# One tile for each PSUM bank, low parts one step later, weight sums one step earlier and a copy moved ahead, in the second feed-forward layer of an encoder step

## The chip, the cores and the metric

The kernel runs on one core of a Trainium2 chip. The metric is the device time of one execution in microseconds (us); smaller is better. Five engines work side by side and wait for each other by semaphores: PE (TensorE, matmuls, with its weight loads shown as PEld), DVE (VectorE), ACT (ScalarE), POOL (GpSimd) and SP (SyncE, which issues the DMA transfers). Matmul results land in PSUM, eight banks of 512 f32 in each of 128 partitions.

## The reference

One layer of a streaming encoder: a SwiGLU feed-forward layer, two attention mixers side by side and a second SwiGLU layer, for 1024 prompt frames and 32 sample frames with 1024 features. The change concerns the second feed-forward layer, on 1056 columns in all:

```
def swiglu(h, w_gate, w_up, w_down):
    return (jax.nn.silu(h @ w_gate) * (h @ w_up)) @ w_down

    h = adaln_in(x, gains[4], sh3, sc3)
    x = x + FFN_RES * g3[:, None] * rmsnorm(swiglu(h, w2_gate, w2_up, w2_down), gains[5])
```

The hidden width is 2816, all data is f32.

## The kernel before

Every matrix product is made of three matmuls of a faster f32 form: each operand is split into a high part (ACT, a copy that rounds) and a low part (DVE, operand minus high part), and the product is high x high + high x low + low x high. A split of 128x512 weights is lines 535 (ACT) and 536 (DVE), in `pair_of`.

The columns are cut into three blocks of 384, 384 and 288. The hidden width is cut into 11 groups of 256. A round takes one group through a gate stage (`g`), an up stage (`u`) and a down stage (`d`); the order of the stages is interleaved, so that round r's down stage follows the gate stage of round r + 1: g(r+1), d(r), u(r+1), g(r+2) and so on. The first two groups are done block by block (six rounds, function `plain`), the other nine for all blocks at once (function `strassen`).

In `strassen` the weights of the group are a 2 x 2 matrix of blocks A11, A12, A21, A22 (128 hidden by 512 input features each), and the first two column blocks with the two halves of the input features form a 2 x 2 matrix too. Seven products in place of eight give the result, with weight sums S1 = A21 + A22, S2 = S1 - A11, S3 = A11 - A21, S4 = A12 - S2 (`Mat.of`, line 559, on DVE) and sums of the input T1 to T4 that are made once. The products run in the order A11, A12, S2, S1, S3, A22, A21, S4. A11, A12, A22 and A21 also make an ordinary product with the third column block (tile `g`, 288 columns); A21 has only that one. The banks are: `a` for A11 and then A12 on top of it, `b` for S2 and then S3, `d` for S1 and then S4, `e` for A22, `0` and `1` for the third block. After A11 the bank `a` is copied out (line 756, ACT), and A12 is added to it. DVE reads `b` after S2, `b` and `d` after S3, `e` after A22 and `d` after S4 (line 741), and `made` turns each finished block into silu (gate, line 688) or into the product with the gate and its split (up: lines 692 on DVE, 693 on ACT, 694 on DVE, tile `gg`).

PSUM is handed out by three pools: `ps2` (two buffers of two banks; before: `b` and `d` together as tile `gu`, the third block's `g`, and the down stage's `dn`), `ps1` (three buffers of one bank; before: `a` and `e`, both named `ge`) and `psc` (one bank). Waits are kept per tile. In SBUF, raw weights have four buffers (tag `r`), split weights four (tag `w`).

The order of the instructions on PE, ACT and DVE is the order of the program from the gate stage of the eighth round (round 7, counted from 0) to the last gate stage (`manual_schedule`); elsewhere a scheduler orders them. In the program, step n of `strassen` splits the weights of products n + 1 and n + 2 before it issues product n; `nexts` loads the next stage's weights after the first product and splits its first ones after the sixth. Low parts are issued right behind their high parts.

Of the kernel before, what the change touches and what calls it, by code (L numbers as in the profile page):

```python
# [10 lines left out]
AF = mybir.ActivationFunctionType  # L11
OP = mybir.AluOpType
# [66 lines left out]
def encoder_step(ctx: ExitStack, tc, x_prompt, x_sample, cache_a_k, cache_a_v, cache_b_k, cache_b_v,  # L79
# [41 lines left out]
    def p2(name, shape=(128, 2, 512)):  # L121
        return ps2.tile(list(shape), F32, name=name, tag="p2")
# [4 lines left out]
    def p1(name, shape=(128, 512)):  # L127
        return ps1.tile(list(shape), F32, name=name, tag="p1")
# [400 lines left out]
        yield from norm_h(f, tb, j + 1, H)  # L529


    def pair_of(src):

        w = t_tile("w", [128, 2, 4, 128], "w", F32R)
        ae.activation(w[:, 0], src, AF.Copy)  # L535
        ve.tensor_tensor(w[:, 1], src, w[:, 0], op=OP.subtract)  # L536
        return w[:, 0], w[:, 1]

    class Mat:
# [19 lines left out]
                ve.tensor_tensor(a[name], x, y, op=op)  # L559
            return a[name]  # L560

        def split(self, name):
            if name not in self.done:
                self.done[name] = pair_of(self.of(name))
            return self.done[name]

    class Rows:
# [9 lines left out]
        def split(self, q, hf):  # L577
            if (q, hf) not in self.w:
                self.w[q, hf] = pair_of(self.raw[q][:, 4 * hf:4 * hf + 4])

    def product(ps, w, x, first, last):
        n = len(x[0])
        for k in range(n):
            for q, (a, b) in enumerate(((0, 0), (0, 1), (1, 0))):
                te.matmul(ps, w[a][:, k, :], x[b][k], start=first and k == 0 and q == 0,  # L585
                          stop=last and k == n - 1 and q == 2, skip_group_check=True)
# [58 lines left out]
    def ffn(key, H, tags, F, facc, wg, wu, wd, key_out, after, beside):  # L645
# [18 lines left out]
            else:  # L664
                loaded[r, what] = Mat((wg, wu)[what == "u"], gi)

        def ready(i):

            if i >= len(stages):
                return  # L670
            load(i)
            r, what = stages[i]
            m = loaded[r, what]
            if what == "d":
                m.split(0, 0)
                m.split(1, 0)
            else:
                m.split("A11")
                if r not in fast or what == "u":
                    m.split("A12")  # L680

        def made(r, what, f, tb, src):

            w = TB[tb][1]
            if what == "g":
                if (r, f, tb) not in sl:
                    sl[r, f, tb] = s_tile([128, 384], "sl")[:, :w]
                ae.activation(sl[r, f, tb], src, AF.Silu)  # L688
# [3 lines left out]
            ve.tensor_tensor(v, v, src, op=OP.mult)  # L692
            ae.activation(g[:, 0, :w], v, AF.Copy)
            ve.tensor_tensor(g[:, 1, :w], v, g[:, 0, :w], op=OP.subtract)  # L694

        def half(tb, d):
            return [e[4 * d:4 * d + 4] for e in H[tb][:2]]

        def plain(r, what, m, tbs, beside, early=None):
            n = 0  # L700
            for f in range(2):
                w_ = [m.split(f"A{f + 1}{d + 1}") for d in range(2)]
                if f and early:
                    early()
                for tb in tbs:
                    w = TB[tb][1]
                    ps = p1("gate" if what == "g" else "up")
                    for d in range(2):
                        product(ps[:, :w], w_[d], half(tb, d), d == 0, d == 1)
                        if f == 0:  # L710
                            m.split(f"A2{d + 1}")
                    made(r, what, f, tb, ps[:, :w])
                    beside(n)
                    n += 1
                    step(STEPS)

        def strassen(r, what, m, two, beside):
            w, w2 = 384, TB[2][1]
            B = {"B11": half(0, 0), "B21": half(0, 1), "B22": half(1, 1), **T}
            banks, v = {}, {}  # L720

            def bank(name):
                if name not in banks:
                    if name in "bd":
                        t = p2("gu")
                        banks["b"], banks["d"] = t[:, 0, :w], t[:, 1, :w]
                    elif name in "01":
                        t = p2("g2")
                        banks["0"], banks["1"] = t[:, 0, :w2], t[:, 1, :w2]
                    else:  # L730
                        banks[name] = p1("ge")[:, :w]
                return banks[name]

            def temp(name, f, tb):
                v[name] = s_tile([128, 384], "sl" if what == "g" else "ut")
                if what == "g":
                    sl[r, f, tb] = v[name]
                return v[name]

            def plus(out, b, x):  # L740
                ve.tensor_tensor(out, banks[b], v[x], op=OP.add)

            seq = [x for x in STRASSEN if two or x[1]]
            for n, (name, x, at, blk2) in enumerate(seq):
                w_ = m.split(name)
                for nx in seq[n + 1:n + 3]:
                    m.split(nx[0])
                if name == "S3":
                    m.of("S4")
                if x:  # L750
                    product(bank(at), w_, B[x], name in ("A11", "S2", "S1", "A22"), True)
                if two and blk2:
                    f, d = int(name[1]) - 1, int(name[2]) - 1
                    product(bank(str(f)), w_, half(2, d), name in ("A11", "A22"), True)
                if name == "A11":
                    ae.activation(temp("s", 1, 0), banks["a"], AF.Copy)
                elif name == "A12":
                    made(r, what, 0, 0, banks["a"])
                elif name == "S2":
                    plus(temp("u", 0, 1), "b", "s")  # L760
                elif name == "S3":
                    plus(v["s"], "b", "s")
                    plus(temp("c", 1, 1), "d", "s")
                    made(r, what, 1, 1, v["c"])
                elif name == "A22":
                    plus(v["s"], "e", "s")
                    made(r, what, 1, 0, v["s"])
                elif name == "S4":
                    plus(v["u"], "d", "u")
                    made(r, what, 0, 1, v["u"])  # L770
                elif name == "A21":
                    made(r, what, 0, 2, banks["0"])
                    made(r, what, 1, 2, banks["1"])
                beside(n)
                step(pace)

        owns = {}

# [36 lines left out]
        steady = ExitStack()  # L815
        for i, (r, what) in enumerate(stages):
            gi, blocks = plan[r]
            if (r, what) == (min(fast) + 1, "g"):
                steady.enter_context(tc.manual_schedule(engines=INLINE))
            if (r, what) == (len(plan) - 1, "u"):  # L820
                steady.close()
            load(i)
            m = loaded[r, what]

            def nexts(n, last, i=i):
                if n == 0:
                    load(i + 1)
                elif n == last:
                    ready(i + 1)

            if what == "d":
                for q in range(2):
                    m.split(q, 0)
                order = list(blocks)
                ending = any(r == final[tb] for tb in order)
                todo = [(tb, mp) for tb in order for mp in range(4)] if ending else \
                    [(tb, mp) for h in range(2) for tb in order for mp in (2 * h, 2 * h + 1)]
                for n, (tb, mp) in enumerate(todo):
                    if n == 1:
                        for q in range(2):  # L840
                            m.split(q, 1)
                    nexts(n, len(todo) - 3)
                    down(r, tb, m, mp)
            elif r in fast:
                need((key, "T"))
                strassen(r, what, m, 2 in blocks, lambda n: nexts(n, 5))
            else:
                for tb in blocks:
# [3 lines left out]
                load(i + 1)  # L852
                plain(r, what, m, blocks, lambda n: None, lambda: ready(i + 1))
            if what == "u" and gi == NF // 2 - 1:
                beside()


    GROUPS = [list(range(g, min(g + 2, NF))) for g in range(0, NF, 2)]

# [807 lines left out]
    def beside():  # L1667
        for t in (1, 0, 2):
            begin(("xp", t), tokens_first(t))
# [36 lines left out]
```

## Time and profile before

| | us |
|---|---|
| median of 3 runs (lowest, highest) | 2240.74 (2239.55, 2245.29) |
| the profiled execution | 2239.8 |
| its span, first to last instruction | 2238.0 |
| block products (first to last matmul of `ge` and `gu`) | 1559.0 to 2182.9 |

The granted TensorE clock over the span is 0.98 of full speed. How to read the rows below: a group has its line, engine, operation, out<-in and count. A row of waits has who waited, for whom, the total, the number of times and the longest. A row in order of time has its start, its length, engine, line and operation, and in brackets how long the engine had stood idle and what released it. The chain of work that ended last has the start, the length and the work on it.

### The profile page before, as it was taken

The page shows a single profiled execution, that of the slowest core. Times are in us where ns is not written, and L with a number is a line of the kernel's source. Part 1 is how long each engine was busy: PE and PEld are TensorE (multiplying, and loading weights), DVE is VectorE, ACT ScalarE, POOL GpSimd, SP SyncE. Part 2 cuts the span into 40 slices and gives each one's busy share as a digit, 9 for nine tenths or more (in the row PEclk, how much of TensorE's full clock was granted, in tenths as well). Part 3 has the DMA queues.
Part 4 walks back from the last instruction along what each step waited for, and adds up shares of the span by engine and source line. Part 5 has one row for each costly group of instructions (what it writes and reads, how often), then busy time and mean ns, then how long its engine had stood idle before and what let it go on. Part 6 is the DMA issues. An engine that isn't in the chain of part 4 may idle for free.

```text
span 2238.0 us, 34284 instructions
## 1 busy us (share of the span) xinstructions
PE 2141.4 (96%) x13796; PEld 2041.0 (91%) x13796; DVE 1406.3 (63%) x2783; ACT 783.3 (35%) x1654; POOL 173.4 (8%) x273
## 2 busy tenths in 40 slices
PE   6999999999999999999999999999999999999997
PEld 4999999999999998898787589999999889998897
DVE  5778667774333596677445866787555555555558
ACT  4412111111111344567445663555322222222224
POOL 1100000000000122001112323210000000000001
PEclk9999999999999999899999999999999999999999
DMA  9244334443121352111103032444211111111114
GB/s 316 99 148 134 102 86 134 129 124 103 40 75 57 118 179 77 37 39 30 54 25 103 5 95 76 144 127 131 62 52 38 57 38 39 55 40 38 38 57 137
DMA packets 178804, 192.35 MB, mean 86 GB/s; under 512 B 7789, under 2 KB 147477, under 8 KB 177493
## 3 DMA queue, kind: packets, MB, share of 16 engines
q1 hardware_dynamic: 178644, 190.16, 27.4%
q8 instruction: 108, 1.77, 0.3%
q14 instruction: 52, 0.42, 0.1%
HBM read 170.42 MB, written 22.86 MB: 86 GB/s over the span
## 4 chain that ended last, share of the span: by engine, by line
PE 83%; DVE 9%; DMA 3%; ACT 3%; issue 1%; POOL 0%; SPq 0%; DVEq 0%; ACTq 0%; POOLq 0%
PE gu L585 6%; PE ge L585 4%; PE g L585 4%; PE up L341 4%; PE gate L341 4%; PE up L340 4%; PE up L339 4%; PE gate L340 4%; PE dn L339 4%; PE dn L340 3%; PE dn L341 3%; PE gate L339 3%; PE dn L795 3%; PE dn L797 3%; PE dn L796 3%; PE po L1060 3%
## 5 line engine op out<-in xcount | busy, mean ns | idle before, releaser
L318 DVE TENSOR_TENSOR w<-raw,w 128x1024 fp32r<-128x1024 f32 x109 | 135.1, 1244 | 81.0 <-ACT w L317 80.1
L795 PE MATMUL dn<-gg,w 128*128 128x384 f32 (+1 forms) x528 | 170.4, 324 | 2.9 <-ACT sl L688 1.4
L382 POOL TENSOR_TENSOR sq<-sq 128x384 f32<-128x384 f32 (+1 forms) x48 | 53.0, 1114 | 1548.0 <-ACT sq L378 1518.3
L339 PE MATMUL dn<-gg,w 128*128 128x384 f32 (+1 forms) x528 | 169.8, 323 | 1.2 <-DVE facc L928 1.1
L796 PE MATMUL dn<-gg,w 128*128 128x384 f32 (+1 forms) x528 | 169.3, 321 | 1.8 <-DVE gg L694 1.8
L340 PE MATMUL dn<-gg,w 128*128 128x384 f32 (+1 forms) x528 | 169.6, 321 | 0.6 <-DVE gg L901 0.6
L341 PE MATMUL dn<-gg,w 128*128 128x384 f32 (+1 forms) x528 | 169.4, 321 | 0.0
L797 PE MATMUL dn<-gg,w 128*128 128x384 f32 (+1 forms) x528 | 168.9, 322 | 0.4 <-DVE w L536 0.4
L317 ACT ACTIVATE w<-raw 128x1024 fp32r<-128x1024 f32 x109 | 114.5, 1056 | 146.0 <-PE up L341 48.8
L535 ACT ACTIVATE w<-raw 128x512 fp32r<-128x512 f32 x180 | 109.0, 624 | 153.7 <-issue 76.0
L802 DVE TENSOR_TENSOR facc<-dn,facc 128x768 f32<-128x768 f32 (+1 forms) x120 | 106.6, 890 | 87.8 <-PE dn L797 87.8
L928 DVE TENSOR_TENSOR facc<-dn,facc 128x768 f32<-128x768 f32 (+1 forms) x120 | 106.1, 887 | 81.3 <-PE dn L341 81.3
L243 DVE SCALAR_TENSOR_TENSOR macc<-raw,csil,macc 128x512 f32<-128x512 f32 x196 | 137.6, 746 | 14.7 <-DMA raw<-in_w_mod_dram 14.4
L536 DVE TENSOR_TENSOR w<-raw,w 128x512 fp32r<-128x512 f32 x180 | 122.8, 706 | 25.1 <-ACT w L535 24.8
L585 PE MATMUL gu<-t,w 128*128 128x384 f32 x648 | 119.7, 336 | 11.2 <-ACT w L535 11.2
L897 ACT ACTIVATE sl<-gate 128x384 f32<-128x384 f32 (+1 forms) x66 | 30.5, 463 | 281.7 <-PE gate L341 278.9
L585 PE MATMUL g<-h_hi,w 128*128 128x288 f32 x576 | 125.8, 298 | 0.0
L585 PEld LDWEIGHTS gu<-t,w 128*128 128x128 f32 x648 | 111.3, 188 | 15.6 <-issue 8.3
L340 PE MATMUL gate<-h,w 128*128 128x384 f32 x352 | 118.0, 335 | 1.9 <-DVE h L467 1.9
L339 PE MATMUL gate<-h,w 128*128 128x384 f32 x352 | 118.3, 336 | 0.0
L341 PE MATMUL gate<-h,w 128*128 128x384 f32 x352 | 117.9, 335 | 0.0
L341 PE MATMUL up<-h,w 128*128 128x384 f32 x352 | 117.9, 335 | 0.0
(314 smaller groups left out, 5820.7 us busy)
## 6 DMA issues: line engine op xcount, KB each, us to landing
raw<-in_w_gate_dram SPq DMA_DIRECT2D x58, 512.0 KB, 4.0
raw<-in_w_up_dram SPq DMA_DIRECT2D x58, 512.0 KB, 4.0
raw<-in_w_down_dram SPq DMA_DIRECT2D x58, 512.0 KB, 3.6
raw<-in_w_mod_dram SPq DMA_DIRECT2D x56, 512.0 KB, 3.9
raw<-in_w_in_dram SPq DMA_DIRECT2D x18, 512.0 KB, 4.2
wm<-in_w_mod_dram SPq DMA_DIRECT2D x8, 1024.0 KB, 7.1
raw<-in_w_out_dram SPq DMA_DIRECT2D x13, 512.0 KB, 4.5
xr<-xs SPq DMA_DIRECT2D x16, 384.0 KB, 3.6
```

Of the source, the lines that this page charges most:

```text
L243: ve.scalar_tensor_tensor(acc[j], r[:, kk], c, acc[j], op0=OP.mult, op1=OP.add)
L317: ae.activation(w[:, 0], r, AF.Copy)
L318: ve.tensor_sub(w[:, 1], r, w[:, 0])
L339: te.matmul(ps, w[:, 0, k], hi, start=start, stop=False)
L340: te.matmul(ps, w[:, 0, k], lo, start=False, stop=False)
L341: te.matmul(ps, w[:, 1, k], hi, start=False, stop=stop)
L535: ae.activation(w[:, 0], src, AF.Copy)
L536: ve.tensor_tensor(w[:, 1], src, w[:, 0], op=OP.subtract)
L585: te.matmul(ps, w[a][:, k, :], x[b][k], start=first and k == 0 and q == 0, stop=last and k == n - 1 and q == 2, skip_group_check=True)
L795: te.matmul(ps[:, s, :w], h[:, k % 4, :], g[:, 0, :w], start=q == 0, stop=False)
L796: te.matmul(ps[:, s, :w], h[:, k % 4, :], g[:, 1, :w], start=False, stop=False)
L797: te.matmul(ps[:, s, :w], l[:, k % 4, :], g[:, 0, :w], start=False, stop=q == 1)
```

## The change

`pair_of` and `made` no longer issue the low part on DVE at once but put it into a list, which `flush` issues at the end of the step. In `strassen`, banks `a`, `b` and `d` are tiles of `ps1` of their own (`ga`, `gb`, `gd`) and `e` is the tile of `psc`. Each step issues its product first; after A11 the copy of bank `a` comes next (new line 774), then the high part of the weights two products on, then the reading of the product before (`after_product`), then the low parts, then the weight sum for the product three on. The next stage's first two weights are split in the last two steps, one each. Down stages take the same form. Loads are issued at the start of a stage. The part in program order begins one round earlier, at the first gate stage in block products.

```diff
+    deferred = []
+
+    def flush():
+        while deferred:
+            deferred.pop(0)()
+
     def pair_of(src):
         w = t_tile("w", [128, 2, 4, 128], "w", F32R)
         ae.activation(w[:, 0], src, AF.Copy)
-        ve.tensor_tensor(w[:, 1], src, w[:, 0], op=OP.subtract)
+        deferred.append(lambda: ve.tensor_tensor(w[:, 1], src, w[:, 0], op=OP.subtract))
         return w[:, 0], w[:, 1]
...
             ae.activation(g[:, 0, :w], v, AF.Copy)
-            ve.tensor_tensor(g[:, 1, :w], v, g[:, 0, :w], op=OP.subtract)
+            deferred.append(lambda: ve.tensor_tensor(g[:, 1, :w], v, g[:, 0, :w], op=OP.subtract))
...
-                    if name in "bd":
-                        t = p2("gu")
-                        banks["b"], banks["d"] = t[:, 0, :w], t[:, 1, :w]
-                    elif name in "01":
+                    if name in "01":
                         t = p2("g2")
                         banks["0"], banks["1"] = t[:, 0, :w2], t[:, 1, :w2]
                     else:
-                        banks[name] = p1("ge")[:, :w]
+                        banks[name] = (pc if name == "e" else p1)("g" + name)[:, :w]
...
-            seq = [x for x in STRASSEN if two or x[1]]
-            for n, (name, x, at, blk2) in enumerate(seq):
-                w_ = m.split(name)
-                for nx in seq[n + 1:n + 3]:
-                    m.split(nx[0])
-                if name == "S3":
-                    m.of("S4")
+            names = [x[0] for x in STRASSEN]
+            for n, (name, x, at, blk2) in enumerate(STRASSEN):
+                w_ = m.done[name]
                 if x:
                     product(bank(at), w_, B[x], name in ("A11", "S2", "S1", "A22"), True)
...
-                if name == "A11":
-                    ae.activation(temp("s", 1, 0), banks["a"], AF.Copy)
-                elif name == "A12":
...
-                beside(n)
+                if n == 0:
+                    ae.activation(temp("s", 1, 0), banks["a"], AF.Copy)
+                if n < 6:
+                    m.begin(names[n + 2])
+                else:
+                    early(n - 6)
+                if n:
+                    after_product(names[n - 1])
+                flush()
+                if n < 5:
+                    m.of(names[n + 3])
                 step(pace)
+            after_product(names[-1])
...
-            if (r, what) == (min(fast) + 1, "g"):
+            if (r, what) == (min(fast), "g"):
+                need((key, "T"))
                 steady.enter_context(tc.manual_schedule(engines=INLINE))
...
             load(i)
             m = loaded[r, what]
+            load(i + 1)
```

Here is ACT where the up stage of round 13 ends and the last gate stage begins, before. `w<-raw` and `w<-ws` are high parts of weights (`ws` is a weight sum), `gg<-sl` high parts of the hidden activations, `sl<-ge` at L756 is the copy of bank `a`; the names after "waits" are the engines waited for.

```order
L693 ACTIVATE gg<-sl 128x288 [waits DVE_49] x2
L693 ACTIVATE gg<-sl 128x384 [waits DVE_49]
L535 ACTIVATE w<-raw 128x512 [waits DMAHW3_49,PE_49,Activation_49]
L535 ACTIVATE w<-ws 128x512 [waits DVE_49,PE_49,Activation_49]
L756 ACTIVATE sl<-ge 128x384 [waits PE_49]
L535 ACTIVATE w<-ws 128x512 [waits Activation_49]
```

And ACT at the same place now; the copy is `sl<-ga` at L774.

```order
L541 ACTIVATE w<-raw 128x512 [waits DMAHW1_49,PE_49,Activation_49]
L699 ACTIVATE gg<-sl 128x288 [waits DVE_49] x2
L699 ACTIVATE gg<-sl 128x384 [waits DVE_49]
L774 ACTIVATE sl<-ga 128x384 [waits PE_49]
L541 ACTIVATE w<-ws 128x512 [waits DVE_49,Activation_49]
L541 ACTIVATE w<-ws 128x512 [waits Activation_49]
```

The copy has moved ahead of the split of S2 (the first `w<-ws`), and the split of A12 (`w<-raw`) ahead of the up stage's last high parts.

DVE at the same boundary, before, from the third block's products with the gate to the low part of S2.

```order
L692 TENSOR_TENSOR sl<-sl,g_19778 128x288 [waits PE_49]
L694 TENSOR_TENSOR gg<-sl,gg 128x288 [waits Activation_49]
L692 TENSOR_TENSOR sl<-sl,g_19778 128x288
L694 TENSOR_TENSOR gg<-sl,gg 128x288 [waits Activation_49]
L741 TENSOR_TENSOR ut<-gu,ut 128x384 [waits PE_49]
L692 TENSOR_TENSOR sl<-sl,ut 128x384 [waits DVE_49]
L694 TENSOR_TENSOR gg<-sl,gg 128x384 [waits Activation_49]
L536 TENSOR_TENSOR w<-raw,w 128x512 [waits DMAHW1_49,Activation_49]
L559 TENSOR_TENSOR ws<-raw 128x512
L559 TENSOR_TENSOR ws<-ws,raw 128x512 [waits DVE_49]
L536 TENSOR_TENSOR w<-ws,w 128x512 [waits Activation_49] x2
```

And DVE there now.

```order
L698 TENSOR_TENSOR sl<-sl,g_19789 128x288 [waits PE_49]
L698 TENSOR_TENSOR sl<-sl,g_19789 128x288
L542 TENSOR_TENSOR w<-raw,w 128x512 [waits DMAHW1_49,Activation_49]
L700 TENSOR_TENSOR gg<-sl,gg 128x288 [waits Activation_49] x2
L744 TENSOR_TENSOR ut<-gd,ut 128x384 [waits PE_49]
L698 TENSOR_TENSOR sl<-sl,ut 128x384 [waits DVE_49]
L565 TENSOR_TENSOR ws<-raw 128x512
L565 TENSOR_TENSOR ws<-ws,raw 128x512 [waits DVE_49]
L700 TENSOR_TENSOR gg<-sl,gg 128x384 [waits Activation_49]
L542 TENSOR_TENSOR w<-ws,w 128x512 [waits Activation_49] x2
```

The low parts (L536, L694; now L542, L700) stand later, with a product or a weight sum between them and the high part that they wait for.

PE in a gate stage before, from A12's product with the third block to S3: `gu<-t_14999` is S2 into bank `b`, `gu<-t_14998` is S1 into bank `d`, `gu<-t_14997` is S3 into bank `b`.

```order
L585 MATMUL gu<-t_14999,w 128x384 [waits DVE_49]
L585 MATMUL gu<-t_14999,w 128x384
L585 MATMUL gu<-t_14999,w 128x384 [waits DVE_49]
L585 MATMUL gu<-t_14999,w 128x384 x9
L585 MATMUL gu<-t_14998,w 128x384 [waits DVE_49,Activation_49]
L585 MATMUL gu<-t_14998,w 128x384 x11
L585 MATMUL gu<-t_14997,w 128x384 [waits Activation_49]
L585 MATMUL gu<-t_14997,w 128x384 x11
```

And PE at the same place now, in tiles `gb` and `gd`.

```order
L595 MATMUL gb<-t_14999,w 128x384 [waits Activation_49]
L595 MATMUL gb<-t_14999,w 128x384
L595 MATMUL gb<-t_14999,w 128x384 [waits DVE_49]
L595 MATMUL gb<-t_14999,w 128x384 x9
L595 MATMUL gd<-t_14998,w 128x384 [waits Activation_49]
L595 MATMUL gd<-t_14998,w 128x384
L595 MATMUL gd<-t_14998,w 128x384 [waits DVE_49]
L595 MATMUL gd<-t_14998,w 128x384 x9
L595 MATMUL gb<-t_14997,w 128x384 [waits DVE_49,Activation_49]
L595 MATMUL gb<-t_14997,w 128x384 x11
```

The first matmul of S1 waited for DVE and now waits for ACT alone (S1's high part); DVE's low part is waited for by the third matmul, which is the first to use it. The wait for DVE's reading of bank `b` stands at S3, which writes that bank.

More of the change, by code (lines that the diff above doesn't have):

```diff
@@ L560, in of, with begin, split @@
             return a[name]
-        def split(self, name):
+        def begin(self, name):
             if name not in self.done:
                 self.done[name] = pair_of(self.of(name))
+        def split(self, name):
+            self.begin(name)
+            flush()
             return self.done[name]
@@ L575, in __init__, with begin @@
                 self.raw.append(r)
-        def split(self, q, hf):
+        def begin(self, q, hf):
             if (q, hf) not in self.w:
@@ L671, in ready @@
             load(i)
[L672 to L676, printed above, removed]
-            else:
-                m.split("A11")
-                if r not in fast or what == "u":
-                    m.split("A12")
+            m = loaded[stages[i]]
+            if stages[i][1] == "d":
+                m.begin(piece, 0)
+            else:
+                m.begin(("A11", "A12")[piece])
         def made(r, what, f, tb, src):
@@ L693, in made, with plain @@
             ae.activation(g[:, 0, :w], v, AF.Copy)
-            ve.tensor_tensor(g[:, 1, :w], v, g[:, 0, :w], op=OP.subtract)
+            deferred.append(lambda: ve.tensor_tensor(g[:, 1, :w], v, g[:, 0, :w], op=OP.subtract))
         def half(tb, d):
             return [e[4 * d:4 * d + 4] for e in H[tb][:2]]
-        def plain(r, what, m, tbs, beside, early=None):
-            n = 0
+        def plain(r, what, m, tbs, early):
             for f in range(2):
                 w_ = [m.split(f"A{f + 1}{d + 1}") for d in range(2)]
-                if f and early:
-                    early()
+                if f:
+                    early(0)
+                    early(1)
+                    flush()
                 for tb in tbs:
@@ L712, in plain, with strassen @@
                     made(r, what, f, tb, ps[:, :w])
-                    beside(n)
-                    n += 1
+                    flush()
                     step(STEPS)
-        def strassen(r, what, m, two, beside):
+        def strassen(r, what, m, early):
             w, w2 = 384, TB[2][1]
@@ L741, in plus, with after_product @@
                 ve.tensor_tensor(out, banks[b], v[x], op=OP.add)
-            seq = [x for x in STRASSEN if two or x[1]]
-            for n, (name, x, at, blk2) in enumerate(seq):
-                w_ = m.split(name)
-                for nx in seq[n + 1:n + 3]:
-                    m.split(nx[0])
-                if name == "S3":
-                    m.of("S4")
[L750 to L754, printed above, removed]
-                if name == "A11":
-                    ae.activation(temp("s", 1, 0), banks["a"], AF.Copy)
-                elif name == "A12":
+            def after_product(name):
+                if name == "A12":
                     made(r, what, 0, 0, banks["a"])
@@ L767, in strassen @@
                     made(r, what, 1, 0, v["s"])
+                elif name == "A21":
+                    made(r, what, 0, 2, banks["0"])
+                    made(r, what, 1, 2, banks["1"])
                 elif name == "S4":
@@ L770, in strassen @@
                     made(r, what, 0, 1, v["u"])
[L771 to L774, printed above, removed]
+            names = [x[0] for x in STRASSEN]
+            for n, (name, x, at, blk2) in enumerate(STRASSEN):
+                w_ = m.done[name]
+                if x:
+                    product(bank(at), w_, B[x], name in ("A11", "S2", "S1", "A22"), True)
+                if blk2:
+                    f, d = int(name[1]) - 1, int(name[2]) - 1
+                    product(bank(str(f)), w_, half(2, d), name in ("A11", "A22"), True)
+                if n == 0:
[6 more added lines that the diff above has]
+                    after_product(names[n - 1])
+                flush()
+                if n < 5:
+                    m.of(names[n + 3])
                 step(pace)
+            after_product(names[-1])
         owns = {}
@@ L823, in ffn @@
             m = loaded[r, what]
[L825 to L829, printed above, removed]
+            load(i + 1)
             if what == "d":
+                ending = any(r == final[tb] for tb in blocks)
+                todo = [(tb, mp) for tb in blocks for mp in range(4)] if ending else \
+                    [(tb, mp) for h in range(2) for tb in blocks for mp in (2 * h, 2 * h + 1)]
                 for q in range(2):
[L833 to L837, printed above, removed]
-                for n, (tb, mp) in enumerate(todo):
[L839 to L842, printed above, removed]
+                    m.begin(q, 0)
+                for n, (tb, mp) in enumerate(todo):
+                    flush()
+                    if n < 2:
+                        m.begin(n, 1)
+                    if n >= len(todo) - 2 and r in fast or r not in fast and n >= 2:
+                        ready(i + 1, n % 2)
                     down(r, tb, m, mp)
             elif r in fast:
-                need((key, "T"))
-                strassen(r, what, m, 2 in blocks, lambda n: nexts(n, 5))
+                for name in ("A11", "A12"):
+                    m.begin(name)
+                strassen(r, what, m, lambda k: ready(i + 1, k))
             else:
+                flush()
                 for tb in blocks:
@@ L851, in ffn @@
                     begin((key, "T"), combos(H, T, tags))
-                load(i + 1)
-                plain(r, what, m, blocks, lambda n: None, lambda: ready(i + 1))
+                plain(r, what, m, blocks, lambda k: ready(i + 1, k))
             if what == "u" and gi == NF // 2 - 1:
                 beside()
+        flush()
     GROUPS = [list(range(g, min(g + 2, NF))) for g in range(0, NF, 2)]
```

2 lines of the change are left out of this document (1 added, 1 removed).

## The prediction

> **What bounds the kernel now.** I read the busy shares of the page first, then who TensorE (PE) waited for in the second feed-forward layer, then one round of that layer on each engine, and last the granted clock around its longest wait.
>
> ```profile
> PE 2141.4 (96%) x13796; PEld 2041.0 (91%) x13796; DVE 1406.3 (63%) x2783; ACT 783.3 (35%) x1654; POOL 173.4 (8%) x273
> 460.00:660.00 200.00, 200.00 (x1254) 199.83 (x1253) 97.28 (x167) 34.56 (x53) 0.00 (x0) 1.00 0.30 90
> 1844.00:1916.00 72.00, 67.03 (x409) 66.21 (x409) 39.73 (x63) 17.71 (x34) 0.00 (x0) 0.98 0.14 45
> PE ge L585 <- ACT sl L756: 24.3, 7, 3.5
> PE gu L585 <- ACT w L535: 11.2, 15, 0.8
> PE dn L795 <- ACT sl L688: 1.4, 2, 0.8
> ```
>
> The first row is the page's busy list: TensorE is the bound, and DVE (VectorE) and ACT (ScalarE) have room. The next two are the table of stretches (length, busy time of PE, PEld, DVE, ACT and POOL, granted clock, DMA share, GB/s). The first feed-forward layer runs TensorE without a gap at clock 1.00; a 72 us stretch of the second, which is about one round, leaves 5 us idle at clock 0.98. The last three are all that TensorE waited for between 1559 and 2183 us, the part in block products: 7 waits of the second product (A12, tile `ge`) for the copy of line 756, and 15 waits on `gu`. Only what shortens these moves the end.
>
> One round, followed back along the chain of work that ended last (start, length, what):
>
> ```profile
> 1900.12 3.83 PE ge L585 x12
> 1903.94 1.59 PE g L585 x12
> 1905.53 2.10 PE gu L585 x12
> 1908.36 4.40 PE gu L585 x24
> 1920.11 0.17 PE dn L795
> 1943.08 2.08 PE ge L585 x12
> 1945.15 1.59 PE g L585 x12
> 1972.15 3.67 PE L585 MATMUL ge<-h,w 128*128 128x384 f32 x12 [3.47 <-ACT sl L756]
> ```
>
> (The last row is from the order of time.) An undisturbed product of 12 matmuls takes 2.08 us at 384 columns and 1.59 us at 288. A gate or up stage has seven of the first and four of the second, 20.92 us; the down stage lasts from 1920.11 to 1943.08, 22.97 us. A round of gate, down and up is then 2 x 20.92 + 22.97 = 64.81 us of work. It took 1972.15 - 1900.12 = 72.03 us. The missing 7.2 us are what the change is aimed at, and they split as follows.
>
> **Part 1, the copy at the head of ACT's order.** Around the same boundary from up to gate:
>
> ```profile
> 1966.69 0.55 DVE L741 TENSOR_TENSOR ut<-gu,ut 128x384 f32<-128x384 f32 x1
> 1967.28 0.56 DVE L692 TENSOR_TENSOR sl<-sl,ut 128x384 f32<-128x384 f32 x1
> 1967.87 0.52 ACT L693 ACTIVATE gg<-sl 128x384 fp32r<-128x384 f32 x1 [1.59 <-DVE sl L692]
> 1968.30 0.61 ACT L535 ACTIVATE w<-raw 128x512 fp32r<-128x512 f32 x1
> 1968.95 0.69 DVE L536 TENSOR_TENSOR w<-raw,w 128x512 fp32r<-128x512 f32 x1
> 1970.28 0.69 DVE L559 TENSOR_TENSOR ws<-ws,raw 128x512 f32<-128x512 f32 x1
> 1971.09 0.63 ACT L535 ACTIVATE w<-ws 128x512 fp32r<-128x512 f32 x1 [2.17 <-DVE ws L559]
> 1971.62 0.47 ACT L756 ACTIVATE sl<-ge 128x384 f32<-128x384 f32 x1
> ```
>
> TensorE had finished A11 and its second-block product at 1972.15 - 3.47 = 1968.68. A12 adds into the same bank and must wait until line 756 has copied it out. The copy itself is 0.47 us, but it stands behind the split of S2, which waited 2.17 us for DVE, which was still working off the up stage. With the copy ahead of that split the 3.47 us go, 24.3 us in seven boundaries. What follows the wait is slow too:
>
> ```profile
> 1900.00:1902.00 2.00, 1.89 (x6) 1.89 (x7) 1.70 (x3) 0.58 (x2) 0.00 (x0) 0.50 0.00 0
> 1902.00:1904.00 2.00, 2.00 (x10) 2.00 (x9) 0.00 (x0) 0.02 (x1) 0.00 (x0) 0.66 0.00 0
> 1682.72 4.21 PE ge L585 x12
> 1686.92 2.27 PE g L585 x12
> 2117.38 3.40 PE ge L585 x12
> 2120.78 2.12 PE g L585 x12
> ```
>
> The granted clock is 0.50 in the two microseconds after the wait. The pairs shown are the first and last of seven; over all seven A12 and the product after it took 40.4 us against 7 x 3.67 = 25.7, so 14.7 us more go with the wait. [...]
>
> Is the copy early enough in the new order? Count from the end of S3's product, with the durations above and DVE's pitch of 0.6 us: two sums out of PSUM, a product with the gate, S4's low part, a low part of `gg`, the sum on `e` with its product, A11's low part, `gg`, make 5.2 us; A21's product ends at 2.08 + 1.59 + 1.59 = 5.26. Then two products at 0.4, A12's low part, two low parts at 0.4: 7.5, after S4's end at 7.34. Sum and product for block 0,1: 8.7; ACT's high copy 0.53: 9.2. A11 ends at 7.34 + 2.08 = 9.42, the copy at 9.9, and A12 can start at 11.0. **1.1 us to spare.** S2's weights come from the two sums (10.0), the split on ACT (10.6) and its low part (11.3), and are wanted at 14.7. So the cover is there; if DVE were later than this by x us, each of the seven boundaries would lose x - 1.1.
>
> **Part 2, a tile for each bank.**
>
> ```profile
> 1907.66 0.56 DVE L741 TENSOR_TENSOR sl<-gu,sl 128x384 f32<-128x384 f32 x1 [1.94 <-PE gu L585]
> 1907.71 0.63 ACT L535 ACTIVATE w<-raw 128x512 fp32r<-128x512 f32 x1 [1.46 <-PE gu L585]
> 1908.36 4.40 PE L585 MATMUL gu<-t,w 128*128 128x384 f32 x24 [0.74 <-ACT w L535]
> 1959.47 0.52 ACT L693 ACTIVATE gg<-sl 128x384 fp32r<-128x384 f32 x1 [6.24 <-DVE sl L692]
> ```
>
> The view puts S1's wait down to ACT's split, but that one is for A21, three products later. S1 writes bank d, half of the tile whose other half, bank b, DVE is reading just then: 1907.66 + 0.56 = 1908.22, and S1 starts 0.14 later. ACT's split ends at 1908.34, 0.02 before S1; the copy of Part 1 ended at 1971.62 + 0.47 = 1972.09 and needed 0.06 to release A12, so 0.02 is too short. The rows of the order agree: S1's first matmul waits for DVE before and no longer afterwards. Gone are 11.2 us in 15 waits. S1 and S3 together took 4.40 after the wait against 2 x 2.08 = 4.16; about 0.23 x 15 = 3.5 us go with it. What is late next is S3, which still waits for DVE's reading of bank b; that is done 0.6 us into S1's 2.08, so nothing shows. Bank d of the next stage needs the last sum of this one, three products earlier; bank e has the one `pc` buffer to itself, a stage apart.
>
> **Part 3, low parts one step later, sums one step earlier.** A low part waits for ACT's high part (0.53 from the row at 1959.47), and DVE waited with it. Now other work stands between. It makes the slack above; by itself it removes nothing that TensorE waits for, so I count nothing. Weights are still split two products ahead, 1.59 + 2.08 = 3.67 us at the least (the next A11), against 0.63 + 0.69 for a split; without that cover a late low part would cost its 0.69 at each product.
>
> **Part 4, loads and the in-order part.** The loads are issued at the start of a stage instead of after its first product. On the queue nothing moves, since it waits for a raw buffer and not for the program's place:
>
> ```profile
> 1909.33 0.69 DVE L559 TENSOR_TENSOR ws<-raw,ws 128x512 f32<-128x512 f32 x1
> 1909.44 0.98 SPq L546 DMA_DIRECT2D raw<-in_w_up_dram  x2
> raw<-in_w_up_dram SPq DMA_DIRECT2D x58, 512.0 KB, 4.0
> ```
>
> The load goes out as the last reader of the buffer starts, a whole down stage (22.97 us) before use, and takes 4.0. The first round of block products now follows the written order too; the plain rounds ahead of it and the closing round are ordered anew by the scheduler. No row shows the new orders:
>
> ```profile
> 1413.00:1559.00 146.00, 142.00 (x877) 138.44 (x876) 129.09 (x249) 81.86 (x148) 16.46 (x13) 1.00 0.45 141
> 1559.00:1631.00 72.00, 70.46 (x449) 69.80 (x448) 39.22 (x69) 25.39 (x48) 0.00 (x0) 1.00 0.21 64
> 2182.00:2238.00 56.00, 44.83 (x305) 42.44 (x304) 45.48 (x104) 26.98 (x50) 8.50 (x9) 0.94 0.43 137
> ```
>
> They could gain at most the idle 4.0, 1.5 and 11.2 us, and lose about as much. The orders differ little in the plain rounds, and in the closing one mainly in where the transposes of the residual stand; I take 0, nearest to the first two rows, and +-6 for the range.
>
> **Sum.** 24.3 + 14.7 + 11.2 + 3.5 = 53.7 us. The profiled execution took 2239.8 (its span is 2238.0 of that), so 2186.1; it lies 0.9 below the median of the runs, 2240.74, so against that median **2187 us**, a factor of 1.025. As a check, the round above would fall from 72.0 to 64.8, and 7.2 us in seven such rounds is 50 of the 53.7.
>
> **Rivals.**
> (a) *The boundary wait shrinks but stays*, because DVE comes later than I counted. With 1 us left per boundary, 7 us stay, and by proportion to the gap 14.7 / 3.47 = 4.2 us of slow clock: 2194 to 2198. DVE would have to be 2.1 us later than counted, over work of 8.7 us made of measured durations. [...] Chance 0.09.
> (b) *The bank tiles do nothing*, because S1 did wait for ACT as the row says: 11.2 + 3.5 stay, 2202. The 0.02 us and the order speak against it. Chance 0.04.
> (c) *The new orders at both ends cost more than 6 us*, say 10: 2197. The closing round has TensorE, DVE and ACT all in its chain. Chance 0.07.
> (d) *Slower: low parts written too late.* Where DVE falls a whole product behind, TensorE stands 2.08 us before S2 and before S4 in each of the 18 stages, 2 x 2.08 x 18 = 75 us: 2187 + 75 = 2262. It decides once DVE lags by more than the 3.4 us that S2's low part has (11.3 against 14.7). DVE is busy 39.7 of 72 us, which speaks against it. Chance 0.03.
> (e) *Nothing happens*, something else holding the boundary: 2240. The chain names this copy in all seven. Chance 0.01.
>
> **How the numbers follow.** The forecast has the remaining 0.76, with 2181 to 2193. The range runs from 2181 to 2199, which takes in most of (a) and (c). A measurement of this kernel can tell about 0.3% from no change, 6.7 us, so (a), (b) and (c) are still faster: faster 0.95, the same 0.02, slower 0.03.
>
> **What would show it.** The wait of A12 for the copy gone from TensorE's list; no stretch between 1650 and 2110 with a clock under 1.00; rounds 64.8 us apart; no wait at the product into bank d. A first product after S2 that still starts 0.7 us late would say (b); a wait for DVE at S2 or S4 would say (d); rounds of 64.8 with a higher total, (c).

## The result, and the profile after

| | before | after |
|---|---|---|
| median of 6 runs, us | 2239.68 (2238.15 to 2245.29) | 2184.83 (2181.91 to 2189.53) |
| profiled execution, us (its span) | 2239.8 (2238.0) | 2184.4 (2182.7) |

The ratio of after to before is 0.9753, with a 95% interval from 0.9738 to 0.9767: 54.9 us fewer. The forecast of 2187 us lies 2.2 us above the median. Between the two profiled executions the difference is 55.4 us.

The page of after: busy time, share of the span and count of each engine.

```profile
PE 2123.9 (97%) x13796; PEld 2029.4 (93%) x13796; DVE 1403.6 (64%) x2783; ACT 786.3 (36%) x1654; POOL 171.8 (8%) x273
```

The counts of instructions are the same on every engine. TensorE is even busy 17.5 us less; the prediction's sum holds 14.7 us of matmuls at a lowered clock and 3.5 of restarts behind waits, 18.2 together. The table of stretches of after (length, busy time and count of PE, PEld, DVE, ACT and POOL, granted clock, DMA share, GB/s):

```profile
1413.00:1559.00 146.00, 141.35 (x877) 138.43 (x876) 127.38 (x246) 80.96 (x147) 16.47 (x13) 1.00 0.45 139
1559.00:1631.00 72.00, 71.20 (x459) 70.97 (x458) 41.50 (x72) 26.11 (x49) 0.00 (x0) 1.00 0.20 68
1650.00:2110.00 460.00, 460.00 (x2899) 460.00 (x2898) 282.76 (x445) 128.60 (x240) 0.00 (x0) 1.00 0.16 49
2128.00:2183.00 55.00, 44.79 (x311) 42.77 (x309) 44.73 (x103) 27.42 (x50) 8.62 (x9) 0.92 0.44 139
```

In the third row TensorE is busy for all of 460 us at clock 1.00. The list of TensorE's waits from 1555 to 2135 us (total, times, longest), the part in block products, has one row left; the waits for the copy of `a` and those on `gu` are gone:

```profile
PE dn L807 <- DVE w L542: 0.8, 1, 0.8
```

One round along the chain of work that ended last (start, length, what):

```profile
1804.61 2.08 PE ga L595 x12
...
1869.45 2.08 PE ga L595 x12
1871.53 1.59 PE g L595 x12
1873.12 2.08 PE ga L595 x12
1875.20 1.59 PE g L595 x12
1876.79 2.08 PE gb L595 x12
1878.88 2.08 PE gd L595 x12
```

A11 of two gate stages stands 1869.45 - 1804.61 = 64.84 us apart; the prediction had 64.81. A12, S2 and S1 take 2.08 us each with nothing between them. The order of time of after at this boundary (brackets: idle time of the engine, and who ended it):

```profile
1870.67 0.53 ACT L699 ACTIVATE gg<-sl 128x384 fp32r<-128x384 f32 x1 [1.97 <-DVE sl L698]
1871.27 0.69 DVE L565 TENSOR_TENSOR ws<-ws,raw 128x512 f32<-128x512 f32 x1
1871.57 0.49 ACT L774 ACTIVATE sl<-ga 128x384 f32<-128x384 f32 x1 [0.37 <-PE ga L595]
1872.06 1.16 ACT L541 ACTIVATE w<-ws 128x512 fp32r<-128x512 f32 x2
1878.71 2.24 PE L595 MATMUL gd<-t,w 128*128 128x384 f32 x12
1878.91 0.56 DVE L744 TENSOR_TENSOR sl<-gb,sl 128x384 f32<-128x384 f32 x1 [2.82 <-PE gb L595]
```

The copy ends at 1871.57 + 0.49 = 1872.06 and A12 starts at 1873.12 by the chain: 1.06 us to spare, where the prediction counted 1.1. (The order of time, in which a product overlaps the end of the one before it, has A12 start 0.17 sooner, at 1872.95.) And S1 (`gd`) starts at 1878.71, before DVE even begins to read bank `b` at 1878.91.

**Where the time went.** The groups of instructions by tile: counts, shortest, median and longest ns, first and last start. The first row is of before, the second of after.

```profile
L585 PE MATMUL gu<-h,w x216: 333/334/446, 1579.7 to 2182.9; 128*128 128x384 f32 x108
```

```profile
L595 PE MATMUL gd<-h,w x216: 334/334/419, 1579.5 to 2129.2; 128*128 128x384 f32 x108
```

This is S4, the last block product of a stage. Its first one starts 0.2 us earlier, its last one 2182.9 - 2129.2 = 53.7 us earlier. The block products thus end sooner by the sum of the prediction. From there to the end of the span it was 55.1 us and is now 53.5: the closing part gives the other 1.6.

### The profile page after: what moved, and what is told of

Same layout as the page of the kernel before. It is cut to its first block, busy times and chain, and to the rows that moved or that the text cites. A ratio compares the mean times of both kernels' runs of the same rounds, so it can differ in the third digit from the quotient of the medians.

```text
span 2182.7 us, 34270 instructions
## 1 busy us (share of the span) xinstructions
PE 2123.9 (97%) x13796; PEld 2029.4 (93%) x13796; DVE 1403.6 (64%) x2783; ACT 786.3 (36%) x1654; POOL 171.8 (8%) x273
## 4 chain that ended last, share of the span: by engine, by line
PE 88%; DVE 6%; DMA 3%; ACT 2%; issue 1%; POOL 0%; SPq 0%; DVEq 0%; ACTq 0%; POOLq 0%
PE g L595 5%; PE dn L339 4%; PE gate L341 4%; PE gate L340 4%; PE dn L340 4%; PE dn L341 4%; PE up L339 4%; PE up L341 4%; PE gate L339 4%; PE up L340 4%; PE ga L595 3%; PE gb L595 3%; PE gd L595 3%; PE dn L807 3%; PE dn L805 3%; PE dn L806 3%
## 5 line engine op out<-in xcount | busy, mean ns | idle before, releaser
L542 DVE TENSOR_TENSOR w<-raw,w 128x512 fp32r<-128x512 f32 x180 | 124.8, 705 | 19.5 <-ACT w L541 19.1
L339 PE MATMUL up<-h,w 128*128 128x384 f32 x352 | 118.1, 335 | 0.0
L341 PE MATMUL up<-h,w 128*128 128x384 f32 x352 | 118.1, 335 | 0.0
L340 PE MATMUL up<-h,w 128*128 128x384 f32 x352 | 117.9, 335 | 0.0
```

What stands on the lines that cost most here:

```text
L339: te.matmul(ps, w[:, 0, k], hi, start=start, stop=False)
L340: te.matmul(ps, w[:, 0, k], lo, start=False, stop=False)
L341: te.matmul(ps, w[:, 1, k], hi, start=False, stop=stop)
L542: deferred.append(lambda: ve.tensor_tensor(w[:, 1], src, w[:, 0], op=OP.subtract))
```

## Experiments: is it the bank tiles that end the wait at S1?

The theory: S1 waited for DVE's reading of the other half of its tile. The rival (b) of the prediction: it waited for ACT's split, as the view says. **After, with banks b and d in one tile again:**

```diff
-                    if name in "01":
+                    if name in "bd":
+                        t = p2("gu")
+                        banks["b"], banks["d"] = t[:, 0, :w], t[:, 1, :w]
+                    elif name in "01":
```

> The changed kernel with banks b and d put back into one two-bank tile; all else as changed. My theory (a shared tile costs a wait of TensorE for DVE's reading): the reading of b now stands behind S1's product in the program, so S1 no longer waits but the reading waits for S1 to end and S3 waits for the reading, 0.56 + 0.15 us, with about 0.23 of restart, in each of 18 stages: +17 us, about 2202. Rival (S1 waited for ACT's split of A21, the tile did nothing): no change, 2185.

Measured: 2201.53 us (2201.26 to 2203.05), ratio to before 0.9832 (0.9814 to 0.985); 16.7 above after. TensorE's waits from 1555 to 2170 us, and one of them in the order of time:

```profile
PE gu L595 <- DVE sl L747: 6.7, 9, 0.7
PE gu L595 <- DVE ut L747: 5.9, 8, 0.7
1889.18 1.11 PE L595 MATMUL gu<-t,w 128*128 128x384 f32 x5 [0.74 <-DVE sl L747]
```

The 0.7 us are back, in 17 waits, and the view names DVE's reading of the tile. But they stand one product further on, at S3. In the new order the reading of bank `b` is issued behind S1's product: S2 and S1 run without a gap, the reading waits for both, and S3 waits for the reading. 12.6 us of waiting and 17 restarts at 0.23 make 16.5. So a tile of two banks costs such a wait in this kernel too; what S1 waited for in the kernel before, this run doesn't show.

That is shown by **before with only the tiles taken apart**:

```diff
-                    if name in "bd":
-                        t = p2("gu")
-                        banks["b"], banks["d"] = t[:, 0, :w], t[:, 1, :w]
-                    elif name in "01":
+                    if name in "01":
...
-                        banks[name] = p1("ge")[:, :w]
+                        banks[name] = (pc if name == "e" else p1)("g" + name)[:, :w]
```

> The kernel before with banks a, b, d as tiles of one bank of their own and e in the one-bank pool; order as before. My theory: the 15 waits of S1 go, 11.2 + 3.5 us, and the boundary stays: about 2225. Rival (S1 waited for ACT): 2240.

Measured: 2221.83 us (2218.78 to 2222.41), ratio 0.9914 (0.9898 to 0.993), 18.4 below before's 2240.20 in that comparison. Its only wait from 1555 to 2170 us is the copy's, unchanged from before:

```profile
PE ga L585 <- ACT sl L753: 24.3, 7, 3.5
```

So the waits at S1 go by the tiles alone, with the old order of ACT and DVE. S1 (`gd`) and ACT's split for A21 in the order of time:

```profile
1897.29 2.24 PE L585 MATMUL gd<-t,w 128*128 128x384 f32 x12
1897.55 0.63 ACT L535 ACTIVATE w<-raw 128x512 fp32r<-128x512 f32 x1 [1.46 <-PE gb L585]
```

S1 starts without a wait, and the split that the view had named starts only behind it. Rival (b) falls.

The gain, 18.4 us, is 3.7 over the 14.7 that was counted. The profiled execution, with 2218.78 us the fastest of the four, is 21.5 us shorter in span than before's. 2.5 of its gain come from the clock: A12 and the product after it took 37.9 us in the seven rounds, 12.2 over 7 x 3.67, where before had 14.7. The closing part gave another 1.9 (from the last start of S4, 2163.3, to the end, 2216.5). Two of the seven A12 along the chain, the one that stayed at full clock and the slowest:

```profile
1749.84 2.38 PE ga L585 x12
...
1888.61 4.21 PE ga L585 x12
```

The gap ahead of both is the same 3.46 us. More on this below.

## Experiments: what ends the wait of A12?

The change moves the copy of `a` ahead of the split of S2, and it puts low parts off. The prediction gave the whole 39 us to the first. Each is undone by itself, then both. **After, with the copy behind the split again:**

```diff
-                if n == 0:
-                    ae.activation(temp("s", 1, 0), banks["a"], AF.Copy)
                 if n < 6:
                     m.begin(names[n + 2])
                 else:
                     early(n - 6)
+                if n == 0:
+                    ae.activation(temp("s", 1, 0), banks["a"], AF.Copy)
```

> The changed kernel with the copy of bank a put back behind the split of S2 on ACT; low parts stay put off. By the profile of the changed kernel the split of S2 could start when its sum is done, 1871.96, the copy would end at about 1873.0 and A12 starts at 1873.1. Theory A (the copy's place and the later low parts each remove the boundary wait by themselves): 2185 to 2187. Theory B (the copy's place is what removes it): the 39 us come back, 2224.

**After, with low parts at once:**

```diff
         ae.activation(w[:, 0], src, AF.Copy)
-        deferred.append(lambda: ve.tensor_tensor(w[:, 1], src, w[:, 0], op=OP.subtract))
+        ve.tensor_tensor(w[:, 1], src, w[:, 0], op=OP.subtract)
...
             ae.activation(g[:, 0, :w], v, AF.Copy)
-            deferred.append(lambda: ve.tensor_tensor(g[:, 1, :w], v, g[:, 0, :w], op=OP.subtract))
+            ve.tensor_tensor(g[:, 1, :w], v, g[:, 0, :w], op=OP.subtract)
```

> The changed kernel with every low part issued right behind its high part again; the copy stays ahead. Theory A (each part is enough alone): 2185 to 2188, the copy waiting only for the last high part of the up stage. Theory C (the later low parts are what removes the wait): most of the 39 us come back, 2215 to 2224. Low parts that TensorE waits for would show as a wait for DVE at S2 or S4.

**After, with both of these edits:**

> Both undone, bank tiles and the rest as changed. A, B and C all expect the boundary wait back. A12's split is earlier than in the kernel before, so DVE comes to S2's sum about 0.7 us sooner: a gap of 2.7 to 3.5 us in seven or eight boundaries, 19 to 28 us, and with the slow clock behind it up to 43: 2204 to 2228. If it stays near 2185, none of the two parts matters and something else in the change removed the wait.

Measured, the three in one comparison, with the median of after from above:

| low parts | copy ahead | copy behind |
|---|---|---|
| one step later | 2184.83 (after) | 2186.78 (2185.28 to 2189.70) |
| at once | 2186.85 (2185.08 to 2187.66) | 2220.59 (2215.98 to 2221.97) |

The ratios to before are 0.9766 (0.975 to 0.9781) with the copy behind, 0.9763 (0.9748 to 0.9779) with low parts at once, and 0.9912 (0.9896 to 0.9927) with both. With the rest of the change in place, either move by itself takes the wait away; only without both does it come back. The copy and A12 in the order of time, first with the copy behind:

```profile
1872.81 0.63 ACT L541 ACTIVATE w<-ws 128x512 fp32r<-128x512 f32 x1 [0.89 <-DVE ws L565]
1873.34 0.47 ACT L778 ACTIVATE sl<-ga 128x384 f32<-128x384 f32 x1
1873.87 2.35 PE L595 MATMUL ga<-h,w 128*128 128x384 f32 x12
```

Then with low parts at once:

```profile
1872.76 0.47 ACT L774 ACTIVATE sl<-ga 128x384 f32<-128x384 f32 x1
1873.28 2.38 PE L595 MATMUL ga<-h,w 128*128 128x384 f32 x12
```

In both the copy ends some 0.05 us before A12 starts: it is just in time, with nothing to spare. The 1 us of slack in after is what the second move adds to the first. A12's matmuls span 2.35 to 2.38 us here instead of 2.08, in eight gate stages, and 8 times 0.28 is about the 2 us by which both medians lie above after's. (The intervals of the ratios overlap with after's, so the times alone don't part these three.) With both undone the copy is late, by the list of waits and by the chain:

```profile
PE ga L595 <- ACT sl L778: 22.5, 8, 2.8
1685.95 2.37 PE ga L595 x12
1753.89 4.21 PE ga L595 x12
2034.20 2.38 PE ga L595 x12
```

Why the low parts' order matters here is seen at the weight sum for S2, first with both undone, then with the copy behind:

```profile
1892.22 0.69 DVE L565 TENSOR_TENSOR ws<-ws,raw 128x512 f32<-128x512 f32 x1
1872.00 0.69 DVE L565 TENSOR_TENSOR ws<-ws,raw 128x512 f32<-128x512 f32 x1
```

With both undone A11's product ended at 1894.09 - 2.81 - 1.59 = 1889.69, and the sum was ready 3.22 us later; ahead of it DVE had stood idle for three of ACT's high parts, 0.51, 0.51 and 0.59 us. With the copy behind but the low parts later A11 ended at 1872.25, and the sum was ready 0.44 us after it.

**Before, with only the copy moved ahead:**

```diff
-                for nx in seq[n + 1:n + 3]:
+                for nx in seq[n + 1:n + (3 if n else 2)]:
                     m.split(nx[0])
...
                     ae.activation(temp("s", 1, 0), banks["a"], AF.Copy)
+                    m.split("S2")
```

> The kernel before with one move: after A11's product the copy of bank a is issued ahead of the split of S2 (in program order it still follows the split of A12). Theory A (the copy's place is enough alone): the copy follows A12's split on ACT, and A12 now waits for DVE's low part of A12, 1968.95 + 0.69 = 1969.64 against 1968.68, so about 1 us is left in seven boundaries and the clock stays up: 24.3 + 14.7 - 7 = 32 us less, about 2208; the 0.7 us waits at S1 stay. Rival C (without putting the low parts off the boundary wait stays): 2236 to 2240.

Measured: 2208.27 us (2207.23 to 2210.22), ratio 0.9854 (0.9837 to 0.9872). Its waits at the products:

```profile
PE gu L585 <- ACT w L535: 11.2, 15, 0.8
PE ge L585 <- ACT sl L756: 4.6, 7, 0.7
```

The wait of A12 falls from 3.5 to 0.7 us but stays. The time is the expected one, the reason isn't: A12 does not wait for the low part of its weights. The copy now stands behind the split of A12 on ACT (1883.80 + 0.61 in the order of time), ends at 1884.33 + 0.47 = 1884.80, and A12 starts at 1884.85; the low part is done only at 1885.14. The loss at S1 is untouched, 11.2 us. **Before with both moves, tiles apart and the copy ahead** (the edits above together), leaves out the low parts' order, the earlier split of A12, the earlier weight sums, the earlier loads and the earlier start of the written order:

> The kernel before with both moves, the copy ahead of the split of S2 and the banks in tiles of their own; low parts, sums and A12's split stay where they were. If the parts add up: 2208 less 11.2 + 3.5, 2193 to 2194, with the 0.66 us wait of A12 left in seven boundaries (4.6 + 2.0 us) as the difference to the changed kernel. If putting off the low parts is worth more than that, it stays above 2196; if A12's wait goes as well, it reaches 2185.

Measured: 2189.18 us (2188.3 to 2192.03), ratio 0.9771 (0.9755 to 0.9787); some 4 us under what was expected. The tiles took 19.1 us off before with the copy ahead (2208.27), about the 18.4 that they gave by themselves, where the expectation had 14.7; so less is left for the rest of the change. It has the wait of before with the copy ahead, and nothing else of weight:

```profile
PE ga L585 <- ACT sl L753: 4.7, 7, 0.7
1873.05 2.39 PE L585 MATMUL ga<-h,w 128*128 128x384 f32 x12 [0.67 <-ACT sl L753]
```

These 4.7 us, with 7 restarts of 0.3, are what the rest of the change still removes: 6.8 us. Between the up stage's last high part and the copy ACT still splits A12 here (0.61 us); after with low parts at once has that split earlier, and no such wait. The kernel lies only 4.4 above after, since its block products start sooner; its group of S4 has its first start 2.0 us ahead of after's, and its last 3.8 behind:

```profile
L585 PE MATMUL gd<-h,w x216: 331/334/422, 1577.5 to 2133.0; 128*128 128x384 f32 x108
```

## Experiment: does the earlier start of the written order cost or gain?

**After, with the part in the written order starting a round later, as before:**

```diff
             if (r, what) == (min(fast), "g"):
                 need((key, "T"))
+            if (r, what) == (min(fast) + 1, "g"):
                 steady.enter_context(tc.manual_schedule(engines=INLINE))
```

> The changed kernel with the in-order part beginning at round 7's gate stage as before, so that the scheduler orders the first round of block products. My theory counted nothing for this: 2183 to 2187, with the round's idle time about 1 us as in the kernel before. Rival (the in-order round is worth several us): 2188 to 2195.

Measured: 2184.32 us (2183.05 to 2185.4), ratio 0.9745 (0.973 to 0.9759), the same as after within the intervals. The 0 that the prediction took stands.

## Experiments: what does a wait cost in clock?

To see what a gap ahead of A12 does, **after with the copy of `a` made several times in each gate stage**, six times and nine times. The further copies write the same values again; the last one comes later.

```diff
-                    ae.activation(temp("s", 1, 0), banks["a"], AF.Copy)
+                    temp("s", 1, 0)
+                    for _ in range(6 if what == "g" else 1):
+                        ae.activation(v["s"], banks["a"], AF.Copy)
```

> The changed kernel with the copy of bank a made six times in each gate stage of block products (the same result), to make a known gap before A12: five more copies at about 0.4 us less the 1.0 us of slack are a gap of about 1.1 us in nine stages. If the clock falls only after gaps near 3.4 us: 9 x (1.1 + 0.2) = 12 us more, about 2197, every A12 at 2.1 to 2.4 us. If slow matmuls follow any gap in proportion (14.7 us to 24.3 us of gap): 6 us on top, 2203.

> The same with nine copies: a gap of about 2.3 us in nine stages. If the clock falls only after gaps near 3.4 us: 9 x 2.5 = 22 us more, about 2207. The kernel with both parts undone had gaps of 2.8 us and A12 at 3.9 to 4.2 us after five of seven of them and at 2.4 after two, so the clock may fall after some of these gaps: up to 9 x 1.9 = 17 us on top, 2224.

Measured, one run each: 2199.43 and 2216.13 us. The order of time with six copies:

```profile
1563.74 2.38 PE L595 MATMUL ga<-h,w 128*128 128x384 f32 x12 [1.60 <-ACT sl L776]
```

With nine:

```profile
1565.24 4.21 PE L595 MATMUL ga<-h,w 128*128 128x384 f32 x12 [3.17 <-ACT sl L776]
1620.69 2.36 PE L595 MATMUL ga<-h,w 128*128 128x384 f32 x12 [3.17 <-ACT sl L776]
```

A copy behind another takes 0.52 us, not the 0.4 that I had put, so six made a gap of 1.60 and not 1.1, and nine one of 3.17 and not 2.3; both expectations miss for this reason. Six copies cost 14.6 us: 9 gaps of 1.60 are 14.4 and 9 restarts at 0.3 are 2.7, less 2.3 by which the block products start sooner in this run (1558.64 against 1560.98 along the chain). Every A12 took 2.38, the length that goes with clock 1.00 in the second stretch below, so the clock did not fall behind any of the nine; its mean over the span is 0.986, and 0.985 in after. With nine, one A12 took 4.21 and the other eight 2.36 to 2.38, though all nine gaps are alike. Two stretches of 2 us of that run, with the clock in the third column from the right:

```profile
1565.50:1567.50 2.00, 2.00 (x7) 2.00 (x8) 1.76 (x3) 0.72 (x2) 0.00 (x0) 0.50 0.00 0
1826.00:1828.00 2.00, 2.00 (x14) 2.00 (x13) 1.89 (x3) 0.56 (x2) 0.00 (x0) 1.00 0.03 8
```

All runs taken together, by the length of A12 behind a wait (2.36 to 2.38 us where the clock stayed up, 3.14 to 4.21 where it had fallen):

| kernel | gap, us | A12 with the clock up, us | A12 with the clock fallen, us | clock fell |
|---|---|---|---|---|
| after, six copies | 1.60 | 2.38 | none | 0 of 9 |
| after, low parts at once and copy behind | 2.81 | 2.37 to 2.38 | 3.91 to 4.21 | 5 of 8 |
| after, nine copies | 3.17 | 2.36 to 2.38 | 4.21 | 1 of 9 |
| before, tiles apart | 3.47 | 2.38 | 3.14 to 4.21 | 6 of 7 |
| before | 3.47 | none | 3.40 to 4.21 | 7 of 7 |

## Why the prediction was right, point by point

**The sum.** 53.7 us were predicted for the block products and 53.7 came; the closing part, counted at 0 with 6 us either way, gave 1.6. To the tenth this is luck: the 14.7 us of slow clock are those of one execution, and before with its tiles apart lost 12.2 behind gaps of the same length. Of the 2.2 us by which the forecast misses, 1.1 come from before itself, whose median was 2240.74 in the prediction and 2239.68 beside the changed kernel. Rivals (c) and (d) fall with it: no row shows a wait for a low part but the one `dn` of 0.8 us.

**The copy, 24.3 and 14.7 us.** The size was right: the wait is gone, the clock is 1.00 through the rounds, and the slack is 1.06 where 1.1 was counted. The copy starts when A11 ends, so this slack is the third block's product of 1.59 less the copy. What the count over DVE and ACT had to show is that ACT is free by then: it had 9.2 against 9.42, 0.2 us early, and the copy's row above has ACT idle for 0.37 us. So DVE could have been about 1.3 us late before TensorE lost anything, a little more than the 1.1 that the prediction allows. That is why rival (a), the wait that shrinks but stays, was unlikely. Rival (a) is what before with the copy ahead does: 0.7 us per round stay.

**The attribution was wrong in one step.** "It makes the slack above; by itself it removes nothing that TensorE waits for, so I count nothing", the prediction says of the low parts. The slack is right: with low parts at once it is gone. The table of the two moves shows the rest to be wrong: with the copy left behind the split, the low parts' order alone takes the time from 2220.59 to 2186.78. In the old order DVE stood waiting for ACT's high parts (0.51, 0.51 and 0.59 us above), and the last low part stood ahead of the sum for S2; the sum came late, and with it the split and the copy behind it. Either the copy steps out of that line, or the line moves faster. The total holds because the two don't add: in the changed kernel each is worth some 34 us without the other, and 2 us with it. In the kernel before, the copy's move alone was worth 32.

**The bank tiles, 11.2 and 3.5 us.** Right in mechanism and size: 18.4 us go when only they are parted, and 16.7 come back when they are joined (at S3, in the new order). What carried it was the arithmetic on end times: a releaser that ends 0.02 us before the start is too late to be the releaser, when the same engine's signal was seen to need 0.06.

**The slow clock.** The 14.7 us went with the gap: A12 takes 2.08 us in after, at clock 1.00. The runs with gaps bear on how it goes where a gap is only shorter. By proportion, 1.60 us gaps would have cost 1.60 / 3.47 of 14.7, 6.8 us in seven; they cost nothing in clock. So the 4.2 us that rival (a) adds by proportion for gaps of 1 us is an estimate that no run bears out. The other reading, in the expectations, was that the clock falls only after gaps near 3.4 us, such as the 3.47 of before. It doesn't hold either: gaps of 2.81 us dropped the clock in 5 of 8.

**The new start of the written order, 0.** Confirmed, by the run that puts it back. The earlier loads and the earlier weight sums have no run of their own, so what each is worth is not shown.

## What to carry to other kernels

Read a wait's named releaser against the end times of all that could hold it: the latest end is not the cause if it is nearer to the start than that engine's signal takes (0.02 us against 0.06 here), and a tile shared by two banks is then the first suspect. Where two edits both loosen one wait, undo them one at a time and together: the first takes nearly all, whichever it is, and the second buys slack. Price a wait on TensorE together with the matmuls behind it, as the trace shows them: here seven waits of 3.47 us cost 24.3 + 14.7, nine of 1.60 us cost no slow clock, and of those of 2.81 and 3.17 us some did and some did not.

## What the runs showed that I had not expected

The length of a gap near 3 us doesn't settle whether the granted clock falls: 3.17 us did it in 1 of 9 and 2.81 in 5 of 8. Two stretches of after with both moves undone, each inside an A12 that had waited 2.81 us. The first A12 starts at 1685.95 and takes 2.37 us, the second starts at 1753.89 and takes 4.21:

```profile
1686.00:1688.00 2.00, 2.00 (x12) 2.00 (x13) 1.54 (x3) 0.56 (x2) 0.00 (x0) 1.00 0.00 0
1754.00:1756.00 2.00, 2.00 (x7) 2.00 (x8) 1.48 (x3) 0.56 (x2) 0.00 (x0) 0.50 0.00 0
```

Nor does the length settle what a fall costs. In before all seven gaps are 3.47 us, and the A12 behind them took 3.40 to 4.21. The first 2 us of the first, second and last of them, which took 4.21, 3.62 and 3.40 us:

```profile
1682.72:1684.72 2.00, 2.00 (x6) 2.00 (x7) 1.58 (x3) 0.46 (x1) 0.00 (x0) 0.50 0.00 0
1755.86:1757.86 2.00, 2.00 (x8) 2.00 (x9) 1.59 (x3) 0.47 (x1) 0.00 (x0) 0.68 0.00 0
2117.38:2119.38 2.00, 2.00 (x9) 2.00 (x10) 1.59 (x3) 0.47 (x1) 0.00 (x0) 0.76 0.00 0
```

In the first the clock is at 0.50 from the start of A12. In the other two the mean is 0.68 and 0.76: over a part of these 2 us A12 still ran at a higher clock. And before with its tiles apart lost 12.2 us behind gaps of the length that cost before 14.7. What else than the length decides has no run of its own, so it is not shown.
